# Moving gate blocks between the stages of a diffusion backbone block on one Trainium2 core

## Chip, core and metric

The kernel runs on one core of one Trainium2 chip. The metric is the device time of one execution in microseconds. The engines are TensorE (PE; its weight loads are shown as PEld), VectorE (DVE), ScalarE (ACT), GpSimd (POOL) and SyncE (SP), which here issues almost all DMAs. Each engine works through its own queue in order.

## What is computed

One layer of a hybrid block on 512 latent tokens and 256 context tokens of width 1024. The normed and modulated input `h` goes through one wide projection, whose columns feed three token mixers and the gates:

```python
proj = h @ w_in
p_qkv, p_z, p_ab, p_hy, p_lx, p_ly, p_gate = jnp.split(proj, offsets, axis=-1)
o_dn, ... = delta_net_branch(p_qkv, p_z, p_ab, ...)   # its output is multiplied by silu(p_z)
o_lru, ... = rglru_branch(p_lx, p_ly, ...)
o_hy = hyena_branch(p_hy, ...)
g_dn, g_hy, g_lru = jnp.split(jax.nn.sigmoid(p_gate), N_BRANCH, axis=-1)
merged = g_dn * (o_dn @ w_proj_dn) + g_hy * (o_hy @ w_proj_hy) + g_lru * (o_lru @ w_proj_lru)
```

After it come an output projection, a residual and a ConvFFN. The parts that matter here are `silu(p_z)` and the three sigmoid gates: 4 x 1024 output columns on the 512 latent tokens, in 32 blocks of 128 columns. They depend on `h` alone, so a block can stand anywhere between the norm and the place where its result is used.

## The kernel before

**Matrix products.** A float32 product is made from three products of a rounded high half and a low half (`mm3`, L173 to L175). A projection of one 128-column block (`load_w`, then `project`) loads 512 KB of weights on SP (L168), splits them into a high half (L155 on ACT or L157 on POOL) and a low half (L160, on DVE or POOL), and runs 8 x 3 matmuls of 128x512 for the latent tokens. Raw weights have three buffers, the high and low halves two each.

**Gate blocks.** `gate(z, m)` is one projection into a PSUM bank, one ACT operation from it (L574: Silu for z = 0, Sigmoid for z = 1, DeltaNet's gate; z = 2, Hyena's; z = 3, RG-LRU's), and one store of 256 KB to memory (L575). Later stages load the result. Of the 32 blocks, eight (z = 3) are in the RG-LRU loop. The 24 others are listed in `fill`: twelve stand beside the triangular solves, with the high half on ACT and the low half on POOL, and twelve in the scan, in halves of 12 matmuls.

**Stages around it.** After a prologue (to about 90 us) comes the RG-LRU loop over eight groups `g` of 128 channels (to about 345 us): `lru_in(g + 1)` (projection and convolution of the next group; its split writes the two halves of xs), `lru_gates(g)` (matmuls, eight sigmoids L518 and L519, four tanh L524 and L525), `gate(3, g)`, `lru_decay` (Exp L532 twice, L534 on DVE, L535 on POOL, L536 on ACT, L537 on DVE, square root L539 on ACT), `lru_scan` (L542, L544, L546, L547 on DVE), `lru_y` (L555 to L558), `lru_out` (L562 and L563 on POOL, then a split, L155 on ACT and L160 on DVE, 512 columns). Then come the merge, queries and keys. From about 530 us to 743 us two runs of triangular solves go on DVE, with a list of values and gate blocks (`work`) handed out beside them; `run` takes one item after every third step of the solve, and all that are left when the solve has ended. The second solve ends in matmuls of 32x32 (L853, L857). Then comes the DeltaNet scan of twelve steps (to about 950 us): four of context, eight of latent tokens. A step is L1005 (state times W and Q), L1015 (the triangular inverse), L1023 (the new state, taken up by DVE in L1028), L1035 (the output). A generator gives a half of a gate block at each of two places in a step: after L1015 and at the end. Beside it run the loads of w_mod (L1050), which DVE sums up (L1054); `mod_sum` turns these sums with a few small matmuls. Hyena, the projections and the FFN follow.

**Order.** A scheduler places the instructions of a stage on their engines by priority; in the prologue and on PE in the scan the order is that of the code. In the RG-LRU loop loads and splits of weights for later groups have a higher priority (`ahead`).

Of the kernel before, what the change touches and what calls it, by code (L numbers as in the profile page):

```python
# [17 lines left out]
P = 128  # L18
# [55 lines left out]
def tile_block(ctx: ExitStack, tc: tile.TileContext, I: dict, out: bass.AP, dbg=None, upto=99):  # L74
# [50 lines left out]
    act = nc.scalar.activation  # L125
# [51 lines left out]
    def project(w, outs):  # L177
        project_part(w, outs, 0, KD)
# [281 lines left out]
    mm, dn = Banks([0, 1, 2, 3]), Banks([4, 5, 6, 7])  # L460
# [67 lines left out]
    def lru_decay(gs, bufs):  # L528
        for g, (R, U, T4, T8) in zip(gs, bufs):
            for d in range(2):  # L530
                j = d * 8 + g
                act(R[:, d], R[:, d], AF.Exp, scale=nsp8[:, j:j + 1])  # L532
        for R, U, T4, T8 in bufs:
            stt(T4, R, 1.0, T4, op0=ALU.add, op1=ALU.mult)  # L534
            nc.gpsimd.tensor_scalar(R, T4, -1.0, 1.0, op0=ALU.mult, op1=ALU.add)  # L535
            act(T4, R, AF.Square)  # L536
            stt(T8, T4, 1.0, T8, op0=ALU.add, op1=ALU.mult)  # L537
        for R, U, T4, T8 in bufs:
            act(T8, T8, AF.Sqrt)  # L539
# [29 lines left out]
    def load_gate(z_, m, e_hi="pool", e_lo="dve"):  # L569
        return load_w(I["w_in"][GATES[z_][0] + m], e_hi=e_hi, e_lo=e_lo)  # L570
# [6 lines left out]
    def gate(z_, m, e_hi="pool", e_lo="dve"):  # L577
        w = load_gate(z_, m, e_hi, e_lo)
        pg = mm()
        project(w, [(pg, hh, hl)])  # L580
        gate_store(z_, m, pg)
# [16 lines left out]
    ksr, knr, kdr = ring(3, [143, 140]), ring(3, seq(146, 3, 2)), ring(3, seq(152, 3, 2))  # L598
    qsr, jkr = ring(2, seq(140, 2, 5)), ring(0.5, seq(158, 0.5, 4))
    atr = ring(1, [170, 171])  # L600
    NFILL = 12

    dcw = pv("dn_conv_w").rearrange("p (b j) -> p b j", j=4)
    kdd = dr.tile([2, TT, P, NH, P], F32, name="kdd")
# [25 lines left out]
    for g in range(8):  # L630
        ahead[0] = g > 0
        if 0 < g < 7:
            ins.append(lru_in(g + 1))
        bufs = lru_gates(g, *ins[g])
        gate(3, g)
        lru_decay([g], [bufs])
        lru_scan(*bufs)
        if g == 7:
            sqs.append(query(0))
        y, u = lru_y(g)  # L640
        lru_out(g, y, u, bufs[2])
        if g == 0:
            after(mark)
            if upto == 0:
                return
# [275 lines left out]
            if each and (not gens or n % EVERY == 0):  # L921
                each.pop(0)()

    fill = [(z_, m) for z_ in range(3) for m in range(8)]
    EVERY, NW1 = 3, 12
    vss = {}

# [5 lines left out]

    values = [lambda h=h: values_(h) for h in range(9)]
    ur = ring(2, [152, 154])
    gates = [lambda f=f: gate(*f, "act", "pool") for f in fill[:NFILL]]
    work = [w_ for p_ in zip(values, gates) for w_ in p_] + values[len(gates):] + gates[len(values):]
    run([solve_first(0), solve_first(1)], work[:NW1])
    run([solve_second()], work[NW1:])
# [12 lines left out]


    ur = ring(2, [186, 188])
    mm = Banks([0])
    o = at(60, [P, 4, NH, P])
    S = [at(84 + 4 * d, [P, NH, P]) for d in range(2)]
    war = ring(4, seq(92, 4, 4))
# [96 lines left out]

    def mod_sum(q):
        if q in (1, 2):
            mp = mm([P, 8])
            for b in range(8):
                mmul(mp[:, b:b + 1], acc[:, b * P:(b + 1) * P], ones[:, 0:1], start=True, stop=True)  # L1060
            vtt(mod34[:, q - 1], mp, pv("b_mod")[:, 16 + q * 8:24 + q * 8], op=ALU.add)
        else:
            row, brow = wr([1, D]), wr([1, D])
            load(brow, I["b_mod"][:, (2 + q) * D:(3 + q) * D])
            for b in range(2):
                mp = mm([1, 512])
                mmul(mp, ones[:, 0:1], acc[:, b * 512:(b + 1) * 512], start=True, stop=True)
                vtt(row[:, b * 512:(b + 1) * 512], mp, brow[:, b * 512:(b + 1) * 512], op=ALU.add)
            load(modr[0 if q == 0 else 1].unsqueeze(0), row)
# [9 lines left out]
    first_ins = len(bb.instructions)  # L1079
    halves = (None for z_, m in fill[NFILL:] for _ in gate_halves(z_, m))  # L1080
    ngap, FBM = 2 * (24 - NFILL), 1
    gap = 0
# [18 lines left out]
    mm, dn = Banks([0, 1, 2]), Banks([3, 4, 5, 6, 7])  # L1101
# [243 lines left out]
    mm = Banks([0, 1, 2, 3])  # L1345
# [263 lines left out]
```

## Time and profile before

| | us |
|---|---|
| median of 3 runs | 1673.54 (1671.61 to 1678.89) |
| profiled execution, its own time | 1676.85 |
| span of its trace | 1675.1 |
| PE busy | 1529.7 (91%) |
| DVE busy | 1195.7 (71%) |
| ACT busy | 615.7 (37%) |
| POOL busy | 589.3 (35%) |

The span is the time between the first and the last instruction of the trace. Busy shares are means over stages with different limits, so a stage is read by its own stretch of the trace: which engine is full there, and if none is, who waits for whom. In a row of a timeline the first number is the start in us, the second the duration; "x2" means that two operations were put together, and the bracket at the end gives the engine's idle time ahead of it and what ended it.

### The profile page before, as it was taken

Reading aid. Unit: us, or ns where it says so; the run is one execution under the profiler, and the core shown is the slowest. Engines: PE = TensorE matmul, PEld = TensorE weight load, DVE = VectorE, ACT = ScalarE, POOL = GpSimd, SP = SyncE. Lnnn points to the kernel's source line nnn. Section 1 sums busy time; section 2 is a strip of 40 time slices with the busy share of each in tenths; the row PEclk is TensorE's granted clock in tenths of the full one; section 3 lists DMA queues with packets and bytes.
Section 4 is the critical chain, followed back from the end, with each engine's and each line's share of the span. In section 5 each row is a group of like instructions: output and inputs, shape, how many; then the busy total and the mean of one; then the engine's idle time right before and its main releaser. Section 6 shows DMA issues by size and latency. Waiting matters only on the chain. (4 is left out here: it accounts for less than half of the span.)

```text
span 1675.1 us, 23659 instructions
## 1 busy us (share of the span) xinstructions
PE 1529.7 (91%) x9176; PEld 1258.0 (75%) x9176; DVE 1195.7 (71%) x1752; ACT 615.7 (37%) x1011; POOL 589.3 (35%) x401
## 2 busy tenths in 40 slices
PE   6899888889999899887999889999999999999998
PEld 2677777767887777775788678787888788888876
DVE  6877888756656997834666375777766899989873
ACT  4367787734553232320111330333222433333311
POOL 4653534325444360312434114222321233334441
PEclk9899999999999896878899999999999999999999
DMA  9432222335344332577888736322462223232331
GB/s 343 162 107 82 76 76 81 103 104 175 127 126 125 110 101 74 173 211 206 233 227 244 253 109 231 107 88 84 162 207 64 68 96 97 92 101 98 104 113 50
DMA packets 93056, 225.66 MB, mean 135 GB/s; under 512 B 9963, under 2 KB 30699, under 8 KB 92176
## 3 DMA queue, kind: packets, MB, share of 16 engines
q1 hardware_dynamic: 92112, 217.86, 41.6%
q0 software_dynamic: 832, 6.29, 0.9%
q8 instruction: 72, 1.18, 0.3%
q14 instruction: 40, 0.33, 0.1%
HBM read 190.45 MB, written 33.66 MB: 134 GB/s over the span
## 5 line engine op out<-in xcount | busy, mean ns | idle before, releaser
L173 PE MATMUL bank<-region,region 128*128 128x512 f32 (+1 forms) x2032 | 761.8, 376 | 28.9 <-DVE region L487 6.8
L175 PE MATMUL bank<-region,region 128*128 128x512 f32 (+1 forms) x2032 | 755.2, 373 | 25.1 <-DVE region L160 22.1
L174 PE MATMUL bank<-region,region 128*128 128x512 f32 (+1 forms) x2032 | 757.2, 373 | 4.2 <-DVE region L160 2.1
L173 PEld LDWEIGHTS bank<-region,region 128*128 128x128 f32 x2032 | 389.7, 192 | 106.8 <-ACT region L155 10.4
L175 PEld LDWEIGHTS bank<-region,region 128*128 128x128 f32 x2032 | 389.5, 192 | 98.6 <-DVE region L160 28.6
L174 PEld LDWEIGHTS bank<-region,region 128*128 128x128 f32 x2032 | 390.6, 192 | 69.0 <-DVE region L418 4.4
L160 DVE TENSOR_TENSOR region<-region,region 128x1024 fp32r<-128x1024 f32 (+2 forms) x241 | 268.7, 1128 | 174.1 <-ACT region L155 98.2
L155 ACT ACTIVATE region<-region 128x1024 fp32r<-128x1024 f32 (+2 forms) x209 | 178.4, 865 | 422.9 <-PE bank L174 132.8
L160 POOL TENSOR_TENSOR region<-region,region 128x1024 fp32r<-128x1024 f32 (+1 forms) x64 | 157.3, 2463 | 237.9 <-ACT region L155 200.4
L157 POOL TENSOR_SCALAR region<-region 128x1024 fp32r<-128x1024 f32 (+1 forms) x96 | 114.3, 1193 | 330.4 <-PE bank L174 147.7
L1423 DVE SCALAR_TENSOR_TENSOR region<-bank,pc,region 128x441 f32<-128x441 f32 (+2 forms) x352 | 224.8, 688 | 4.3 <-ACT region L1412 0.7
L485 DVE SCALAR_TENSOR_TENSOR region<-bank,pc,region 128x511 f32<-128x511 f32 (+1 forms) x56 | 34.1, 629 | 48.7 <-ACT region L482 45.8
L1054 DVE SCALAR_TENSOR_TENSOR region<-region,cc,region 128x1024 f32<-128x1024 f32 x28 | 41.7, 1488 | 33.9 <-DMA region<-in_w_mod_dram 33.4
L992 POOL TENSOR_TENSOR region<-region,region 128x512 f32<-128x512 f32 x32 | 49.1, 1564 | 39.5 <-DMA region<-rowd 36.8
L482 ACT ACTIVATE region<-bank,pc 128x512 f32<-128x512 f32 (+1 forms) x40 | 23.1, 597 | 98.6 <-PE bank L175 98.6
L1435 POOL TENSOR_TENSOR region<-region,region 128x512 f32<-128x512 f32 x22 | 34.3, 1561 | 66.3 <-DVE region L1423 52.3
L1028 DVE SCALAR_TENSOR_TENSOR region<-region,egl,bank 128x128 f32<-128x128 f32 x160 | 42.3, 339 | 21.3 <-PE bank L1023 21.3
L1005 PE MATMUL bank<-region,region 128*64 128x128 f32 x608 | 42.4, 306 | 9.2 <-DVE region L1028 9.2
L1005 PEld LDWEIGHTS bank<-region,region 128*64 128x64 f32 x608 | 39.8, 157 | 14.4 <-DVE region L1028 6.4
L1017 ACT ACTIVATE region<-bank 128x512 f32<-128x512 f32 x24 | 14.3, 598 | 89.9 <-PE bank L1015 89.9
L574 ACT ACTIVATE region<-bank 128x512 f32<-128x512 f32 x32 | 18.8, 588 | 70.6 <-PE bank L175 66.4
L1137 POOL TENSOR_TENSOR region<-region,region 128x512 f32<-128x512 f32 x8 | 12.2, 1523 | 85.6 <-DVE region L1121 85.6
(275 smaller groups left out, 1669.7 us busy)
## 6 DMA issues: line engine op xcount, KB each, us to landing
region<-in_w_in_dram SPq DMA_DIRECT2D x97, 512.0 KB, 3.9
region<-in_w_mod_dram SPq DMA_DIRECT2D x48, 512.0 KB, 6.2
region<-in_ffn_up_dram SPq DMA_DIRECT2D x44, 512.0 KB, 3.5
region<-in_w_proj_dram SPq DMA_DIRECT2D x24, 512.0 KB, 3.6
region<-in_ffn_down_dram SPq DMA_DIRECT2D x22, 512.0 KB, 3.5
gated<-region SPq DMA_DIRECT2D x32, 256.0 KB, 2.1
region<-gated SPq DMA_DIRECT2D x32, 256.0 KB, 4.0
kdd<-region SPq DMA_DIRECT2D x16, 384.0 KB, 2.8
```

The source lines that it names most:

```text
L155: act(hi, raw, AF.Copy)
L157: nc.gpsimd.tensor_scalar(hi, raw, 1.0, 0.0, op0=ALU.mult, op1=ALU.add)
L160: (vtt if e_lo == "dve" else gtt)(lo, raw, hi.bitcast(F32), op=ALU.subtract)
L173: mmul(ps, lh, rh, start=start, stop=False)
L174: mmul(ps, lh, rl, start=False, stop=False)
L175: mmul(ps, ll, rh, start=False, stop=stop)
L992: gtt(wq[d][:, hs], KQ[hf][:, :, chs[d] - 4], eg[:, hs].unsqueeze(2).to_broadcast([P, 4, 2, 64]), op=ALU.mult)
L1005: mmul(X[hf][rcs[d], h, :], wq[d][:, hf * 4 + h, kind], S[d][:, hf * 4 + h, :], start=(kind == 0 or h == 0), stop=(kind == 0))
L1028: stt(S[d][:, h], S[d][:, h], egl[:, d, c, i, h:h + 1], p3[hf][d][:, h % 4], op0=ALU.mult, op1=ALU.add)
L1054: stt(acc, w_, cc[:, k, 0:1], acc, op0=ALU.mult, op1=ALU.add)
L1423: stt(uv[:, ro, co], pv_[:, ri, ci], w[:, a * 3 + b:a * 3 + b + 1], uv[:, ro, co], op0=ALU.mult, op1=ALU.add)
L1435: gtt(uu[0], uu[0], uu[1], op=ALU.mult)
```

## The change

The list `fill` begins with z = 1 now. Its first eight blocks go into the RG-LRU loop, one in each iteration right behind `gate(3, g)`, with both halves of the weights split on POOL. The next ten (eight of z = 0, two of z = 2) stand beside the solves instead of twelve. Six are left for the scan instead of twelve; `ngap` follows from `NFILL`, so that a half comes only in every second place, the one at the end of a step. `mod_sum` writes to PSUM bank 1 instead of bank 0, which it shared with the gate halves.

```diff
-    NFILL = 12
+
+    NEARLY, NMERGE, NSOLVE = 8, 0, 10
+    NFILL = NEARLY + NMERGE + NSOLVE
+    fill = [(z_, m) for z_ in (1, 0, 2) for m in range(8)]
...
         gate(3, g)
+        if g < NEARLY:
+            gate(*fill[g], "pool", "pool")
         lru_decay([g], [bufs])
...
-    fill = [(z_, m) for z_ in range(3) for m in range(8)]
     EVERY, NW1 = 3, 12
...
-    gates = [lambda f=f: gate(*f, "act", "pool") for f in fill[:NFILL]]
+    gates = [lambda f=f: gate(*f, "act", "pool") for f in fill[NFILL - NSOLVE:NFILL]]
...
-    mm = Banks([0])
+    mm, mm1 = Banks([0]), Banks([1])
...
-            mp = mm([P, 8])
+            mp = mm1([P, 8])
...
-                mp = mm([1, 512])
+                mp = mm1([1, 512])
```

Lines behind the first of these places have a number some 3 to 5 higher in the changed kernel (L853 is L858 there, L1017 is L1021).

On ACT in the RG-LRU loop, before: the end of one group's tanh (L524, L525), with the copy of xs (L155, 128x768) and the out-copy (L155, 128x512) among them, the gate's sigmoid (L574), and the decay.

```order
L155 ACTIVATE region_800<-region_83 128x768
L525 ACTIVATE region_1068<-region_1065,sp_744 128x768
L524 ACTIVATE region_1067<-region_1065,sp_745 128x768
L155 ACTIVATE region_106<-region_1353 128x512
L525 ACTIVATE region_1068<-region_1065,sp_744 128x768
L574 ACTIVATE region_1491<-bank_63 128x512
L532 ACT_TABLE_LOAD
L532 ACTIVATE region_1065<-region_1065,nsp_746 128x768 x2
L555 ACTIVATE region_992<-bank_64 128x512
L557 ACT_TABLE_LOAD
L557 ACTIVATE region_992<-region_992 128x512
L536 ACTIVATE region_1067<-region_1065 128x1536
```

The same place in the changed kernel, from the first sigmoids (L518, L519) of the group to its first tanh:

```order
L518 ACTIVATE region_1095<-bank_69,pc 128x256
L518 ACTIVATE region_1096<-bank_69,pc 128x256
L519 ACTIVATE region_1095<-bank_70,pc 128x512
L155 ACTIVATE region_106<-region_1441 128x512
L519 ACTIVATE region_1096<-bank_67,pc 128x512
L518 ACTIVATE region_1095<-bank_68,pc 128x256
L519 ACTIVATE region_1095<-bank_69,pc 128x512
L518 ACTIVATE region_1096<-bank_68,pc 128x256
L519 ACTIVATE region_1096<-bank_70,pc 128x512
L524 ACTIVATE region_1097<-region_1095,sp_745 128x768
```

The out-copy has moved from a place behind all sigmoids and three of the tanh to one behind three sigmoids. And on ACT from the last tanh of that group on, in the changed kernel:

```order
L525 ACTIVATE region_1098<-region_1095,sp_744 128x768
L532 ACT_TABLE_LOAD
L532 ACTIVATE region_1095<-region_1095,nsp_746 128x768
L574 ACT_TABLE_LOAD
L574 ACTIVATE region_1163<-bank_66 128x512
L532 ACT_TABLE_LOAD
L532 ACTIVATE region_1095<-region_1095,nsp_746 128x768
L574 ACT_TABLE_LOAD
L574 ACTIVATE region_1193<-bank_63 128x512
L536 ACTIVATE region_1097<-region_1095 128x1536
L555 ACTIVATE region_1022<-bank_64 128x512
L539 ACT_TABLE_LOAD
```

The two gates' operations (L574) now stand between and behind the two Exps, each with a table load of its own, and the square root's table load comes right behind L555.

On ACT at the end of the solves, before: the last gate blocks (L155 splits their weights, L574 is their Silu or Sigmoid) ahead of the first copies L854 of the second solve's matmuls.

```order
L155 ACTIVATE region_697<-region_436 128x1024
L574 ACT_TABLE_LOAD
L574 ACTIVATE region_3961<-bank_63 128x512
L155 ACTIVATE region_437<-region_696 128x1024
L574 ACTIVATE region_4084<-bank_64 128x512
L574 ACTIVATE region_3961<-bank_65 128x512
L574 ACTIVATE region_4084<-bank_66 128x512
L854 ACTIVATE region_4852<-bank_67 32x512
```

The same place in the changed kernel (L897 copies a value, L859 is L854 before):

```order
L155 ACTIVATE region_437<-region_696 128x1024
L574 ACTIVATE region_4316<-bank_66 128x512
L897 ACTIVATE region_3393<-bank_69 128x256
L897 ACTIVATE region_3393<-bank_70 128x512
L574 ACT_TABLE_LOAD
L574 ACTIVATE region_4193<-bank_63 128x512
L574 ACTIVATE region_4316<-bank_64 128x512
L859 ACTIVATE region_5084<-bank_67 32x512
```

Of the four blocks behind the last value, two are left.

On PE in a latent step of the scan, before, from L1015 over the half block (12 matmuls, of which the last five stand here) to L1023:

```order
L1015 MATMUL bank_65<-region_1354,region_5718 64x128 x8
L1015 MATMUL bank_66<-region_2456,region_5718 64x128 x8
...
L174 MATMUL bank_63<-region_81,region_437 128x512
L175 MATMUL bank_63<-region_80,region_438 128x512
L173 MATMUL bank_63<-region_80,region_437 128x512
L174 MATMUL bank_63<-region_81,region_437 128x512
L175 MATMUL bank_63<-region_80,region_438 128x512
L1023 MATMUL bank_69<-region_1175,region_5480 128x128
L1023 MATMUL bank_70<-region_1175,region_5480 128x128
```

The same place in the changed kernel (L1019 is L1015 before, L1027 is L1023):

```order
L1019 MATMUL bank_65<-region_1442,region_5753 64x128 x8
L1019 MATMUL bank_66<-region_2688,region_5753 64x128 x8
L1027 MATMUL bank_69<-region_1235,region_5571 128x128
L1027 MATMUL bank_70<-region_1235,region_5571 128x128
L1027 MATMUL bank_69<-region_1235,region_5571 128x128
L1027 MATMUL bank_70<-region_1235,region_5571 128x128
```

The half is gone from between them; the one at the end of a step stays.

## Rows read from the trace of the kernel before

**Rows 1.** The page: its head, and what the DMAs moved in 40 slices.

```profile
span 1675.1 us, 23659 instructions
GB/s 343 162 107 82 76 76 81 103 104 175 127 126 125 110 101 74 173 211 206 233 227 244 253 109 231 107 88 84 162 207 64 68 96 97 92 101 98 104 113 50
```

**Rows 2.** Stretches: us, busy time of PE, PEld, DVE, ACT, POOL, PEclk, DMA share, GB/s.

```profile
145.00:290.00 145.00, 128.28 (x629) 104.23 (x627) 121.57 (x110) 109.46 (x139) 62.78 (x38) 1.00 0.25 80
199.50:226.80 27.30, 24.31 (x121) 19.83 (x121) 23.30 (x22) 21.16 (x28) 11.73 (x7) 1.00 0.23 77
700.00:743.00 43.00, 35.41 (x358) 30.56 (x358) 20.54 (x16) 13.46 (x20) 9.28 (x5) 0.78 0.69 199
743.00:811.00 68.00, 52.76 (x452) 41.68 (x452) 36.80 (x70) 9.23 (x16) 15.84 (x14) 0.87 0.76 212
811.00:950.00 139.00, 132.47 (x1474) 112.35 (x1475) 80.07 (x167) 18.93 (x33) 50.93 (x36) 0.95 0.84 231
1450.00:1500.00 50.00, 50.00 (x222) 41.40 (x221) 44.09 (x66) 18.78 (x25) 18.88 (x9) 1.00 0.31 104
```

**Rows 3.** Timeline of ACT in the RG-LRU loop, 199 to 236 us.

```profile
207.21 0.63 ACT L155 ACTIVATE region<-region 128x512 fp32r<-128x512 f32 x1 [4.19 <-POOL region L563]
...
209.18 1.28 ACT L532 ACT_TABLE_LOAD   x1
210.47 1.77 ACT L532 ACTIVATE region<-region,nsp 128x768 f32<-128x768 f32 x2
...
223.07 1.26 ACT L519 ACTIVATE region<-bank,pc 128x512 f32<-128x512 f32 x2
...
226.08 0.97 ACT L524 ACTIVATE region<-region,sp 128x768 f32<-128x768 f32 x1
...
234.61 0.63 ACT L155 ACTIVATE region<-region 128x512 fp32r<-128x512 f32 x1 [4.20 <-POOL region L563]
```

**Rows 4.** Timeline of DVE in the same stretch.

```profile
212.27 1.76 DVE L534 SCALAR_TENSOR_TENSOR region<-region,region 128x1536 f32<-128x1536 f32 x1 [1.66 <-ACT region L532]
...
222.05 1.74 DVE L542 TENSOR_TENSOR region<-region,region 128x1536 f32<-128x1536 f32 x1
...
230.27 3.16 DVE L160 TENSOR_TENSOR region<-region,region 128x1024 fp32r<-128x1024 f32 x2
```

**Rows 5.** Timeline of POOL in the same stretch.

```profile
230.50 2.12 POOL L562 TENSOR_TENSOR region<-region 128x512 f32<-128x512 f32 x1 [2.42 <-ACT region L524]
232.69 1.89 POOL L563 TENSOR_TENSOR region<-region,region 128x512 f32<-128x512 f32 x1
```

**Rows 6.** Timeline of POOL beside the solves, 580 to 620 us.

```profile
582.95 13.91 POOL L160 TENSOR_TENSOR region<-region,region 128x1024 fp32r<-128x1024 f32 x2 [8.29 <-ACT region L155]
...
616.44 2.40 POOL L160 TENSOR_TENSOR region<-region,region 128x1024 fp32r<-128x1024 f32 x1 [3.97 <-ACT region L155]
```

**Rows 7.** Timeline of PE behind the RG-LRU loop, 336 to 344 us.

```profile
342.70 0.39 PE L667 MATMUL bank<-ident,region 32*128 32x32 f32 x2 [5.94 <-ACT region L662]
```

**Rows 8.** Timelines of DVE, PE and ACT at the end of the second solve.

```profile
711.24 2.07 DVE L839 STREAM_TRANSPOSE region<-region 32x1024 f32<-32x1024 f32 x1
...
725.93 1.26 PE L853 MATMUL bank<-region,region 32*32 32x32 f32 x34
...
726.09 0.60 ACT L574 ACTIVATE region<-bank 128x512 f32<-128x512 f32 x1 [4.84 <-PE bank L175]
```

**Rows 9.** Timeline of the scan's context steps, 786 to 797 us, all engines.

```profile
792.17 1.04 POOL L157 TENSOR_SCALAR region<-region 128x1024 fp32r<-128x1024 f32 x1 [5.17 <-DMA region<-in_w_in_dram]
793.25 1.23 DVE L160 TENSOR_TENSOR region<-region,region 128x1024 fp32r<-128x1024 f32 x1 [2.60 <-POOL region L157]
...
795.05 2.19 PE L1005 MATMUL bank<-region,region 128*64 128x128 f32 x18 [6.01 <-DVE region L1028]
```

**Rows 10.** Timeline of a latent step of the scan, 848 to 860 us, PE.

```profile
851.71 1.96 PE L1015 MATMUL bank<-region,region 64*64 64x128 f32 x32
...
856.55 2.06 PE L1023 MATMUL bank<-region,region 64*128 64x128 f32 x32
```

## Prediction

> **What bounds the kernel now.** Read the page first. The span is 1675.1 us and the profiled execution took 1676.85 us; the 1.75 us between them lie outside the program and stay. The sum is made against that execution; the median of the three runs shown, 1673.54 us, is 3.3 us lower, and the sum is carried over to it unchanged.
>
> Next, the table of stretches [rows 2]: in the tail of the program (1450 to 1500) TensorE (PE) is busy for all of 50.00 us, so whatever the stages before give or lose passes through to the end. Three of them hold gate blocks that the change moves. In the RG-LRU loop, 27.3 us for one of the eight channel groups hold PE 24.31, DVE 23.30, ACT 21.16: no engine is full. From 700 to 743 PE is busy 35.41 of 43 us; in the scan 52.76 of 68 us (context steps) and 132.47 of 139 (latent steps).
>
> Then the ACT queue of the loop [rows 3]. The copy that makes the high half of the branch's output (L155, 512 columns; the out-copy from here on) starts at 207.21 and at 234.61, 27.40 us apart, and both times ACT has waited 4.2 us for POOL's L563. So the loop is set by a chain through all engines: out-copy, sigmoid of the gate and Exp on ACT (210.47), L534 on DVE (212.27), L535 to L542 (222.05) [rows 4], the scans, POOL's L562 and L563 (230.50, 232.69) [rows 5], out-copy. It reaches the end: at 342.70 PE has stood 5.94 us for an ACT copy, L662, that is queued behind the last out-copy [rows 7].
>
> **Price of a gate block.** 222 matmuls of 512 columns took 50.00 us [rows 2], 0.225 us each; a block has 24 of them, 5.4 us of PE. On ACT it adds a sigmoid of 0.6 us [rows 8], on SP two issues (a load of 512 KB, a store of 256 KB), and two splitting operations that now go to POOL: 1.04 us for the high half [rows 9], 2.40 for the low half where DVE leaves POOL alone, and 13.91 for two, 7 each, beside the solves [rows 6].
>
> **Part 1, eight blocks into the loop.** If PE were the limit, eight blocks would cost at most 43 us, and a period could not fall below 24.31 + 5.4 = 29.7 us. But the chain is what counts, and the ACT order changes on it at two places. First, the out-copy of the group before is now queued after three of the eight sigmoids of the next group, where it came after all of them and most of the tanh. So ACT's work that today fills the time before the copy has to wait behind it. Second, the new gate's sigmoid parts the two Exps, so that three table loads stand ahead of the second Exp instead of one.
>
> I count from the end of the out-copy to L534. Before: 234.61 less 27.40 is 207.21, plus 0.63 is 207.84; L534 starts at 212.27: 4.4 us. After: five sigmoids, which with one more take 226.08 - 223.07 = 3.0 us before [rows 3], so 2.4; four tanh and the copy of xs, some 0.85 each by L524's 0.97 less its overlap with the next, 4.2; three table loads at 1.28, 3.85; a sigmoid 0.6; two Exps 1.77 [rows 3]. That is 12.9 us, **8.5 more**. From L534 to L542 it is now 9.8 us [rows 4]; afterwards the table load of the square root stands before the wait, with no convolution work between, and it lies under DVE's L537: 8.4 is my estimate, 1.4 less. From L542 to the end of the out-copy it is now 13.2 us; afterwards DVE does its third scan before the rest of the convolution and the split: 11.5, 1.7 less. The period becomes 27.4 + 8.5 - 1.4 - 1.7 = 32.8 us, 5.4 more, over the 29.7 that PE needs. Six periods of that are 32 us, and the last, which has no convolution to wait for, I put at 3: **+35 us**, and PE passes it on at L662. The bounds are 7 x (29.7 - 27.3) = +17, if ACT's waits close up until PE is the limit, and +57 (the third rival). I take the chain, since its rows are the ones that PE waits for. POOL's new work (3.4 us a block, 8 at the worst price) lies between L563 and L535, some 15 us; SP's sixteen issues lie in a stretch with a DMA share of 0.25 [rows 2]; but the two stores of a period now wait on SP for the second gate sigmoid, 13 us after the out-copy, and the next loads stand behind them. Three raw weight buffers are filled ahead, 16 us of PE, so I cost that at nothing; without that cover a load comes late in each period, which the upper bound takes in.
>
> Table loads are where the Trainium skill speaks against the change. At 209.18 the load takes 1.28 us, and the Exp starts at 210.47, right behind it [rows 3]. The Trainium skill, "ScalarE: Activation LUTs", section "What ACT_TABLE_LOAD costs", adds a drain of about 1.38 us to every switch; the two more loads on the chain would then cost 2.8 us a period more, some 19 us in all. The trace shows no such gap, and I leave it out.
>
> **Part 2, ten blocks beside the solves instead of twelve.** The order moves nothing until the end, where four blocks run in a row, and after the change two. DVE finishes its part of the second solve at 711.24 + 2.07 = 713.3; PE comes to L853, which needs it, at 725.93, right behind the last block, whose sigmoid is at 726.09 [rows 8]. Two blocks less are 2 x 5.4 = **-11 us**, to 715.1, still 1.8 us behind DVE, so nothing else becomes late by the rows. The bounds are -5, if the loads or POOL's splits hold up the earlier blocks, and -12.6, DVE's finish. The loads of w_mod that were fetched there, at 199 GB/s [rows 2], start as much earlier.
>
> **Part 3, six blocks in the scan instead of twelve.** Every step had a half block between L1015 and L1023 and another after L1035; the first goes. L1015 ends at 851.71 + 1.96 = 853.7 and L1023 starts at 856.55 [rows 10]; between them PE did the half, 2.9 us. L1023 needs ACT's copies of L1015's two results (L1017), and the first of them can be made while the second result is still computed, so hardly anything on PE's own path fills that gap again: twelve halves are 35 us, the best case. Against it stand the loads. The scan moves 212 and 231 GB/s at shares of 0.76 and 0.84 [rows 2], 46.5 MB. Six blocks take 4.7 MB from that: 1.6 MB at 212 GB/s and 3.1 MB at 231 are **21 us**, if the scan goes with its bytes. DVE shows how loads reach PE: a half's raw weights came late (POOL waited 5.17 us, 792.17), the split followed on DVE (793.25), and L1028 behind it in the same queue held PE for 6.01 us (795.05) [rows 9]. Such waits belong to the load order, and fewer blocks don't remove all of them. I take **-25**, nearer to the bytes than to PE. The worst case counts the blocks as cheap bytes, at the highest rate of the page, 343 GB/s [rows 1]: -14. mod_sum's new bank frees it from the gate's bank at four places; it waits instead for L1028 to have read bank 1, for which L1005 right behind it waits anyway: I cost that at nothing.
>
> **Sum.** +35 - 11 - 25 = -1: 1675.9 in terms of the profiled execution, **1672.5 us** in terms of the median.
>
> **The rivals.** *The loop is held by PE after all.* Then ACT's out-copy doesn't wait, since the chain has room, and part 1 costs 17: 1654.5. For it: PE is the busiest engine there, at 24.31. Against it: the 4.2 us that ACT waits each time. 12%.
>
> *The scan goes down to PE's floor*, -35: 1662.5. For it: latent steps leave PE idle for 6.5 of 139 us only. Against it: a DMA share of 0.84. 15%.
>
> *POOL's splits hold up DVE.* In the loop two DVE splits beside POOL's L562 took 3.16 us (230.27) [rows 4], 1.58 each against 1.23 [rows 9], and L562 itself 2.12; beside the solves a split of POOL takes 7 us instead of 2.4 [rows 6]. After the change POOL starts the new block's splits right behind L563, while DVE does the out-split, the rest of the convolution and, behind them, what ACT's xs copy waits for; that copy has hardly 0.3 us to spare in the count above. If DVE stands for all of POOL's 1.04 + 2.40 us, 3.1 come through in each of seven periods, +22: 1694.5, slower. It decides from about 1 us a period. Against it: DVE's operations grew by 0.35 us, not by POOL's whole time. 10%. The Trainium skill, "SBUF — State Buffer" section "SBUF: two separate sides",, calls the port that both use an exclusive lock for a whole instruction, where DVE reads two operands from SBUF; the 7 us agree with that for POOL.
>
> *The scan stays with its loads*, -14: 1683.5, slower. For it: DVE and POOL wait for loads there (5.17 us at 792.17), and PE without a half to do waits in its place. 17%.
>
> That the blocks don't move is excluded by the order. **Chances and range.** My forecast has 46%. 0.5% (8.4 us) is about what a measurement of this kernel can tell from no change: the edges are 1665.2 and 1681.9. Faster: 12 + 10 of the 15 + 7 of my own = 29%. Slower: 10 + 12 of the 17 + 4 = 26%. The rest, 45%, is within. The range holds the forecast, the scan's two cases and the edge of the first rival: 1654 to 1692.
>
> **What would show it.** In the loop the out-copies should stand 32 to 33 us apart, with five sigmoids behind each and no wait of ACT for PE; 29 to 30 apart with PE full is the first rival, 35 or more with longer DVE splits the third. PE's wait for the last out-copy, which ends at 342.70 now, should end near 378. L858 (L853 before) should start within 2 us of DVE's last transpose. The scan, from there to the end of its last state update, should be 25 us shorter; PE's time between L1019 and L1027 should be near zero. I am wrong if ACT finds room for the sigmoids before the out-copy, or if clock or loads in the scan take back the halves.

## The result, and the profile after

The changed kernel took 1701.1 us (median of 4 runs, 1698.07 to 1707.22) against 1674.68 us before (4 runs, 1671.61 to 1678.89): a ratio of **1.0138**, 95% interval 1.011 to 1.0167. By the ratio it is slower by some 23 us (the two medians are 26 apart), where 1672.5 was forecast and 1692 was the upper end. The profiled execution has a span of 1701.0 us, 25.9 more than before [rows 1]. The sums below are made between the two profiled executions.

The stretches of the changed kernel that answer to [rows 2], in the same columns: one whole stretch of the RG-LRU loop, one period of it, the end of the solves, context and latent steps of the scan, and 50 us of the tail.

```profile
145.00:290.00 145.00, 133.35 (x634) 110.53 (x633) 98.38 (x92) 110.50 (x137) 68.56 (x41) 0.98 0.28 91
199.50:232.50 33.00, 30.46 (x144) 25.35 (x144) 22.31 (x22) 24.38 (x31) 15.25 (x9) 0.95 0.26 88
742.00:776.00 34.00, 23.93 (x310) 21.12 (x310) 21.76 (x20) 10.25 (x16) 3.44 (x2) 0.75 0.59 171
776.00:842.00 66.00, 50.99 (x528) 42.23 (x530) 36.33 (x74) 9.23 (x16) 13.55 (x13) 0.82 0.79 224
842.00:979.00 137.00, 104.38 (x1248) 90.03 (x1244) 68.57 (x157) 15.99 (x26) 38.27 (x31) 0.86 0.78 206
1475.00:1525.00 50.00, 50.00 (x222) 41.38 (x221) 44.07 (x66) 18.06 (x24) 18.91 (x9) 1.00 0.32 101
```

The tail is as full as before. The scan is the surprise: its latent steps take 137 us where they took 139, with 28 us less of PE's busy time in them, and TensorE's granted clock fell from 0.95 to 0.86.

To see where time goes, I compare the start of the same instruction in both traces: the first transpose behind the loop (L667, now L672), the first of the keys' squares (L760, L765), DVE's last transpose of the solves (L839, L844), the last 32x32 product (L853, L858), and the first transpose of Hyena (L1141, L1145).

| place | before | after | shift | of that in the part |
|---|---|---|---|---|
| first transpose behind the RG-LRU loop | 342.7 | 380.1 | +37.4 | +37.4 loop |
| first of the keys | 449.4 | 491.6 | +42.2 | +4.8 merge and queries |
| DVE's last transpose of the solves | 711.2 | 756.3 | +45.1 | +2.9 keys and solves |
| last 32x32 product | 735.0 | 768.5 | +33.5 | -11.6 end of the solves |
| first transpose of Hyena | 976.6 | 1001.3 | +24.7 | -8.8 scan |
| span | 1675.1 | 1701.0 | +25.9 | +1.2 the rest |

**The loop.** ACT, DVE and POOL in one period of the changed kernel (the places of [rows 3 to 5]):

```profile
211.18 0.63 ACT L155 ACTIVATE region<-region 128x512 fp32r<-128x512 f32 x1 [6.02 <-POOL region L563]
...
218.32 1.28 ACT L532 ACT_TABLE_LOAD   x1
...
220.57 1.28 ACT L574 ACT_TABLE_LOAD   x1
...
222.48 1.28 ACT L532 ACT_TABLE_LOAD   x1
223.78 0.94 ACT L532 ACTIVATE region<-region,nsp 128x768 f32<-128x768 f32 x1
...
244.23 0.63 ACT L155 ACTIVATE region<-region 128x512 fp32r<-128x512 f32 x1 [5.94 <-POOL region L563]
```

```profile
211.84 0.86 DVE L160 TENSOR_TENSOR region<-region,region 128x512 fp32r<-128x512 f32 x1 [1.43 <-ACT region L155]
...
224.75 1.76 DVE L534 SCALAR_TENSOR_TENSOR region<-region,region 128x1536 f32<-128x1536 f32 x1 [5.11 <-ACT region L532]
226.43 1.22 DVE L160 TENSOR_TENSOR region<-region,region 128x1024 fp32r<-128x1024 f32 x1
...
233.85 1.76 DVE L542 TENSOR_TENSOR region<-region,region 128x1536 f32<-128x1536 f32 x1 [0.95 <-ACT region L539]
```

```profile
212.24 2.73 POOL L160 TENSOR_TENSOR region<-region,region 128x1024 fp32r<-128x1024 f32 x1
...
226.59 2.39 POOL L535 TENSOR_SCALAR region<-region 128x1536 f32<-128x1536 f32 x1 [3.38 <-DVE region L534]
```

The out-copies are 33.05 us apart (32.8 in the prediction) and ACT waits 6 us for each of them. From the out-copy's end at 211.81 to L534 it is 12.9 us, as summed; from there to L542 9.1 (8.4 summed); from there to the next out-copy's end at 244.86 11.0 (11.5 summed).

**The scan.** The largest waits of PE and of POOL, each first before (743 to 977 us), then after (776 to 1002 us). The columns: who waited and for whom, us in total, times, the longest.

```profile
PE bank L1005 <- DVE region L1028: 9.2, 3, 6.0
PE bank L1015 <- DVE region L1009: 6.6, 3, 4.5
...
POOL region L992 <- DMA region<-rowd: 36.8, 7, 11.5
```

```profile
PE bank L1009 <- POOL region L996: 37.0, 12, 7.3
PE bank L1071 <- DVE region L1072: 5.9, 2, 5.1
...
POOL region L996 <- DMA region<-rowd: 82.9, 8, 27.2
```

L996 (L992 before) is POOL's product that makes W and Q for a step from the rows `rowd`; L1009 (L1005) is the step's first product on PE. Before, PE seldom waited for that product, since it still had half blocks to do when the rows came. With the half between L1019 and L1027 gone, PE comes to the next step's first product earlier, and there it waits for POOL, 37 us in all, and POOL for the rows.

### The profile page after: what moved, and what is told of

It reads as the page before. It is cut to its first block, busy times and chain, and to the rows that moved or that the text cites. A ratio compares the mean times of both kernels' runs of the same rounds, so it can differ in the third digit from the quotient of the medians.

```text
span 1701.0 us, 23683 instructions
## 1 busy us (share of the span) xinstructions
PE 1541.7 (91%) x9176; PEld 1274.6 (75%) x9176; DVE 1183.8 (70%) x1746; ACT 632.9 (37%) x1024; POOL 597.8 (35%) x409
## 5 line engine op out<-in xcount | busy, mean ns | idle before, releaser
L160 DVE TENSOR_TENSOR region<-region,region 128x512 fp32r<-128x512 f32 (+1 forms) x235 | 264.7, 1137 | 166.8 <-ACT region L155 100.1
L155 ACT ACTIVATE region<-region 128x1024 fp32r<-128x1024 f32 (+2 forms) x207 | 176.5, 864 | 426.2 <-PE bank L174 129.8
L160 POOL TENSOR_TENSOR region<-region,region 128x1024 fp32r<-128x1024 f32 (+1 forms) x70 | 174.2, 2494 | 231.2 <-ACT region L155 195.6
L1009 PE MATMUL bank<-region,region 128*64 128x128 f32 x608 | 51.5, 334 | 37.4 <-POOL region L996 37.0
L1009 PEld LDWEIGHTS bank<-region,region 128*64 128x64 f32 x608 | 46.5, 174 | 45.7 <-POOL region L996 42.4
L996 POOL TENSOR_TENSOR region<-region,region 128x512 f32<-128x512 f32 x32 | 41.5, 1327 | 82.9 <-DMA region<-rowd 82.9
L1021 ACT ACTIVATE region<-bank 128x512 f32<-128x512 f32 x24 | 14.3, 597 | 140.6 <-PE bank L1019 136.5
L1439 POOL TENSOR_TENSOR region<-region,region 128x512 f32<-128x512 f32 x22 | 34.4, 1562 | 66.4 <-DVE region L1427 59.6
L1013 DVE TENSOR_TENSOR region<-region,bank 128x512 f32<-128x512 f32 x22 | 14.8, 685 | 39.0 <-PE bank L1009 34.3
L534 DVE SCALAR_TENSOR_TENSOR region<-region,region 128x1536 f32<-128x1536 f32 x8 | 14.8, 1854 | 37.9 <-ACT region L532 37.9
```

The lines of the kernel that those rows point to most:

```text
L155: act(hi, raw, AF.Copy)
L160: (vtt if e_lo == "dve" else gtt)(lo, raw, hi.bitcast(F32), op=ALU.subtract)
L996: gtt(wq[d][:, hs], KQ[hf][:, :, chs[d] - 4], eg[:, hs].unsqueeze(2).to_broadcast([P, 4, 2, 64]), op=ALU.mult)
L1009: mmul(X[hf][rcs[d], h, :], wq[d][:, hf * 4 + h, kind], S[d][:, hf * 4 + h, :], start=(kind == 0 or h == 0), stop=(kind == 0))
L1439: gtt(uu[0], uu[0], uu[1], op=ALU.mult)
```

## Experiments

Runs of one group share the runs of the kernel before. "Behind the loop" is the start of the first transpose behind the RG-LRU loop, "scan" the time from the scan's first product (L1015 in the kernel before) to Hyena's first transpose, both in us from one trace of each kernel. The scan varies by itself: with the scan of the kernel before it was 233.2 and 228.4 us (before, dup_lru), with that of the changed kernel 224.6, 219.3 and 232.2 (after, d_first, p_first). So a difference under some 13 us between the scans of two single traces is no finding; the ratios rest on several runs each.

| kernel | ratio to before | 95% interval | behind the loop | scan |
|---|---|---|---|---|
| after | 1.0138 | 1.011 to 1.0167 | 380.1 | 224.6 |
| dup_lru | 1.0238 | 1.0196 to 1.0279 | 379.9 | 228.4 |
| scan6 | 0.9942 | 0.9914 to 0.9969 | 343.4 | 221.5 |
| d_first | 1.0071 | 1.005 to 1.0092 | 364.2 | 219.3 |
| p_first | 1.0213 | 1.0181 to 1.0246 | 386.6 | 232.2 |
| r_high | 1.021 | 1.0168 to 1.0252 | 379.4 | 230.6 |
| r_four_high | 1.023 | 1.0198 to 1.0262 | 380.7 | 234.4 |
| nomod | 0.9903 | 0.9872 to 0.9934 | 379.1 | 178.9 |
| mod_small | 0.9942 | 0.9917 to 0.9967 | 380.4 | 187.7 |
| mod_short | 1.0114 | 1.007 to 1.0158 | 379.8 | 217.5 |
| mod_late | 1.0093 | 1.0061 to 1.0126 | 364.3 | 160.1 |
| mod_hy | 0.9916 | 0.9883 to 0.9948 | 367.4 | 159.9 |
| mod_split | 0.9869 | 0.9843 to 0.9896 | 367.5 | 178.1 |

### The loop's part alone: dup_lru

```diff
         gate(3, g)
+        gate(1, g, "pool", "pool")
         lru_decay([g], [bufs])
```

> The kernel before, with eight gate blocks computed once more in the RG-LRU loop, where the change puts them (they are computed again in their old places, so everything behind the loop is as before). It shows what the loop's part costs alone. Theory 1 (a chain over all engines, ACT's queue in it): out-copies 33 us apart, +37 us at the last out-copy, +40 to +43 us in all, since PE loses behind the loop the wait that it had there: 1715 to 1718. Rival (PE holds the loop): out-copies under 30.5 us apart, +17 to +22: 1692 to 1697. The sum of the prediction had +35: 1709.

1717.29 us against 1678.92: +38, and by the ratio +40 (33 to 47). The out-copies were 33.05 us apart, and the first transpose behind the loop came at 379.9. So the loop's part costs what theory 1 says, some 5 more than the prediction's +35; the rival's 17 to 22 is out.

### The scan's part alone: scan6

```diff
-    halves = (None for z_, m in fill[NFILL:] for _ in gate_halves(z_, m))
-    ngap, FBM = 2 * (24 - NFILL), 1
+    halves = (None for z_, m in fill[NFILL:18] for _ in gate_halves(z_, m))
+    ngap, FBM = 12, 1
...
-        load(th, gated[2, m])
+        load(th, gated[2, m % 2])
```

> The kernel before with six gate blocks in the scan instead of twelve, in every second place, and the sums of w_mod in bank 1; six of Hyena's gate blocks are left out and others are read in their place. It shows what the scan's part gives alone. Theory 2 (a step waits for its own row loads, which SP issues late, so that PE idles where the halves stood): the scan's own length within 6 us of before, in all -2 to -10. Rival bytes: -21. Rival PE's floor: -35. The prediction had -25.

1669.6 us: a ratio of 0.9942, -10 us (-5 to -14). Six blocks with 32 us of PE's work went out of the kernel altogether, and it lost 10. Bytes at the scan's mean rate (-21) and PE's floor (-35) are out; the fourth rival's -14 is at the edge. The scan of its trace is 11.7 us shorter than before, where theory 2 had 6 at most. PE's new wait is here too, with nothing changed ahead of the scan:

```profile
PE bank L1005 <- POOL region L992: 27.9, 10, 6.5
```

That the time fits theory 2 doesn't yet show that the late issue of the rows is the cause.

### The order on ACT: d_first and p_first

d_first puts the early gate ahead of lru_gates in the code and makes a group's output behind lru_gates of the next; p_first does the first alone.

```diff
+    held = []
     for g in range(8):
...
+        if g < NEARLY:
+            gate(*fill[g], "pool", "pool")
         bufs = lru_gates(g, *ins[g])
+        if held:
+            lru_out(*held.pop())
         gate(3, g)
-        if g < NEARLY:
-            gate(*fill[g], "pool", "pool")
...
-        lru_out(g, y, u, bufs[2])
+        held.append((g, y, u, bufs[2]))
```

> The changed kernel, where in the loop the early gate block stands ahead of lru_gates and the output of a group is made after lru_gates of the next group in the code. This puts the order on ACT back: the out-copy behind the tanh, both Exps together, four table loads in a group instead of six; PE, POOL and DVE do the same work as in the changed kernel. Theory 1 (the ACT order lengthens the chain): out-copies 29.5 to 31 us apart instead of 33, in all -14 to -24 against the changed kernel, 1677 to 1687. Rival (POOL's splits hold DVE up, or PE's work counts in full wherever it stands): 33 us apart as in the changed kernel, 1698 to 1703.

> The changed kernel with the early gate block ahead of lru_gates in the code, and the output of a group left where it was. On ACT both Exps stand together again and a group has four table loads, but the out-copy stands ahead of all eight sigmoids of the next group. It parts the two causes in the ACT order. Theory 1 by the terms of the sum: from the out-copy's end to L534 11.7 us instead of 12.9, a period of 31 to 32.5 us, in all -4 to -14 against the changed kernel. If the table loads were the whole cause, the period would be 29.7 to 30.5, as in d_first; if the out-copy's place were, 33 as in the changed kernel.

d_first has 1.0071 against the 1.0138 of the changed kernel, 11 us of it regained (the forecast had 14 to 24). ACT and then PE's stretches (columns of [rows 2]) in its loop:

```profile
218.00 0.61 ACT L155 ACTIVATE region<-region 128x512 fp32r<-128x512 f32 x1
...
219.12 1.28 ACT L532 ACT_TABLE_LOAD   x1
220.41 1.77 ACT L532 ACTIVATE region<-region,nsp 128x768 f32<-128x768 f32 x2
...
249.05 0.62 ACT L155 ACTIVATE region<-region 128x512 fp32r<-128x512 f32 x1
```

```profile
199.50:232.50 33.00, 32.81 (x164) 27.55 (x163) 23.49 (x22) 23.16 (x29) 12.93 (x9) 1.00 0.34 111
232.50:265.50 33.00, 31.16 (x147) 25.88 (x147) 23.81 (x22) 23.60 (x32) 13.38 (x9) 0.95 0.28 92
```

The out-copies are 31.05 us apart, ACT no longer waits for POOL at them, and PE is close to full: a loop near the first rival's (29 to 30 us) appears. The first transpose behind the loop comes 15.9 us earlier than in the changed kernel, so the order of the code is worth that much of the 37; the other 21.5 remain with the same blocks in the better order. The edit gives PE, DVE and POOL another order too, so that the whole of the 15.9 comes from ACT is argued from the rows and not shown by itself.

p_first should have kept a part of the gain, by the count; it was slower than the changed kernel, with out-copies 34.2 to 34.5 us apart in the middle of the loop. DVE in it:

```profile
231.20 1.76 DVE L534 SCALAR_TENSOR_TENSOR region<-region,region 128x1536 f32<-128x1536 f32 x1 [1.57 <-ACT region L532]
...
238.32 0.69 DVE L160 TENSOR_TENSOR region<-region,region 128x512 fp32r<-128x512 f32 x1 [2.12 <-POOL region L157]
238.93 1.75 DVE L537 SCALAR_TENSOR_TENSOR region<-region,region 128x1536 f32<-128x1536 f32 x1
...
242.24 1.76 DVE L542 TENSOR_TENSOR region<-region,region 128x1536 f32<-128x1536 f32 x1 [1.56 <-ACT region L539]
```

The out-copy ended at 218.78, so L534 came 12.4 us later: two table loads less on the way saved half a microsecond, since all eight sigmoids stand there now. And from L534 to L542 it is 11.0 us, not 8.4, because a weight split of POOL and then one of DVE stand ahead of L537. So taking away two table loads doesn't shorten the period as long as the out-copy stands ahead of the sigmoids. How much the out-copy's place and the parted Exps are worth alone isn't shown: p_first made the first worse while it mended the second, and d_first mends both.

### Earlier rows: r_high and r_four_high

```diff
+        egs = [None] * 2
+        for d in range(2) if s else ():
+            egs[d] = egr([P, NH, 64])
+            with tc.high_priority():
+                load(egs[d], rowd[1, d, chs[d]].partition_broadcast(P))
         v, kd, wa = chunk_loads(s, lat)
         wq = [None] * 2
         for d in range(2) if s else ():
-            eg = egr([P, NH, 64])
-            load(eg, rowd[1, d, chs[d]].partition_broadcast(P))
+            eg = egs[d]
```

> The changed kernel with the row loads of a scan step issued ahead of its other loads and at a higher priority; bytes, blocks and buffers are the same. Theory 2 (late issue of the row loads on SP): POOL's L996 waits for rowd for less than half of 83 us, PE's L1009 for POOL less than half of 37 us, and the scan is 12 to 22 us shorter: 1679 to 1689. Rival (the DMAs are full, whatever the order): the waits move to other loads and the time stays, 1697 to 1703.

r_four_high takes four buffers instead of `egr`'s two in the latent steps.

> The changed kernel with the row loads of a scan step ahead and at a higher priority, as in r_high, and four buffers for them instead of two in the latent steps, so that SP does not stand behind POOL's use of the old rows. If SP's head-of-line wait for the two buffers (60 us in r_high) is what took r_high's gain away: the wait under 20 us and the scan 10 to 20 us shorter than in the changed kernel, 1681 to 1691. If the loads as a whole hold the scan (theory 3: what SP can issue and the DMAs can land of one step's 2 MB, w_mod's 512 KB blocks among them): PE's wait moves on to the sums of w_mod or to vd and wad, and the time is 1698 to 1713.

Neither is faster than the changed kernel; by the ratios, 1.021 and 1.023, both are slower. In both PE's wait for POOL is gone from the list, and new ones stand there; the largest of PE and of SP in r_high's scan, and that of SP in r_four_high's (L1013 is L1005 before, L1068 the small products of w_mod's sums, L1062 DVE's additions, L991 the issue of the rows, L1000 POOL's product from them):

```profile
PE bank L1068 <- DVE region L1062: 19.6, 2, 11.3
PE bank L1023 <- DVE region L1017: 9.0, 5, 3.7
```

```profile
SPq L991 <- POOL region L1000: 60.5, 12, 15.7
```

```profile
SPq L991 <- POOL region L1000: 65.8, 12, 15.1
```

Theory 2's remedy falls: with the rows ahead, SP stands for POOL, which still reads the old rows, w_mod comes later, and PE waits for its sums. r_four_high was to take that wait of SP away (under 20 us) and didn't: it is 65.8 us with four buffers. So it doesn't tell what room for more rows would give, and an order with the rows early and SP free was not tried. In both orders that were tried, another load is late: that is what theory 3 says.

### What the loads wait for: nomod, mod_small, mod_short

nomod leaves out most of the loads and additions of w_mod; mod_small makes the loads small; mod_short makes the additions short. mod_late, below, moves them all. The edits of nomod, mod_small and mod_short, in that order:

```diff
-        for k in range(4) if s_ % 3 < 2 else ():
+        for k in range(1) if s_ % 3 == 0 else ():
```

```diff
-        load(w_, I["w_mod"][k * P:(k + 1) * P, (2 + q) * D:(3 + q) * D])
+        load(w_[:, 0:128], I["w_mod"][k * P:(k + 1) * P, (2 + q) * D:(2 + q) * D + 128])
```

```diff
-            stt(acc, w_, cc[:, k, 0:1], acc, op0=ALU.mult, op1=ALU.add)
+            stt(acc[:, 0:64], w_[:, 0:64], cc[:, k, 0:1], acc[:, 0:64], op0=ALU.mult, op1=ALU.add)
```

> The changed kernel with 28 of the 32 loads of w_mod in the scan left out, and the additions that use them; blocks, step loads and their order otherwise stay. Theory 3 (the step's loads queue behind w_mod's on SP and in the DMAs): POOL's L996 waits little for rowd, PE's L1009 waits under 10 us for POOL, a latent step takes 11 to 13 us, and the scan is 35 to 55 us shorter than the changed kernel's, 1645 to 1666. Rival (each step's own chain of rows, POOL, PE and DVE sets 16 us): scan shorter by less than 15, 1686 to 1701.

> The changed kernel, where each of the 32 loads of w_mod in the scan brings 64 KB instead of 512 KB; the count of loads, their places on SP, the buffers that they wait for and DVE's 32 full additions stay (the sums are then not w_mod's). It parts w_mod's bytes from its places in the queues. If the bytes hold the scan (the step's own loads wait behind them in the DMAs): nearly the gain of nomod (28 loads and additions left out), the scan 30 to 46 us shorter than in the changed kernel, 1655 to 1671. If the places on SP or DVE's additions hold it: under 12 us shorter, 1689 to 1701.

> The changed kernel with all 32 loads of w_mod whole, but 28 of DVE's additions over 64 columns instead of 1024 (0.2 instead of 1.3 us each; the sums are then not w_mod's). It takes 30 us of work from DVE in the scan and leaves the bytes. If the bytes hold the scan: under 8 us shorter than the changed kernel, 1693 to 1703. If DVE's queue holds it: 15 to 30 us shorter, 1671 to 1686.

nomod's scan is 46 us shorter than the changed kernel's, mod_small's 37, mod_short's 7, which is within the spread. All three lengths and times came out as theory 3, or the bytes, had them; only POOL's own wait for the rows in nomod, 34.2 us, is not as little as was expected. The whole scan as one stretch (columns of [rows 2]) of the kernel before, the changed one, mod_small and mod_short, one fence each:

```profile
743.40:976.60 233.20, 205.31 (x2006) 169.84 (x2006) 130.25 (x250) 46.29 (x122) 70.00 (x51) 0.93 0.78 223
```

```profile
776.70:1001.30 224.60, 175.43 (x1858) 147.97 (x1858) 117.14 (x244) 42.78 (x116) 54.48 (x46) 0.86 0.77 217
```

```profile
778.80:966.50 187.70, 163.25 (x1857) 139.32 (x1857) 123.99 (x242) 42.62 (x116) 61.45 (x46) 0.93 0.72 189
```

```profile
774.90:992.40 217.50, 174.07 (x1858) 147.94 (x1858) 93.17 (x244) 42.77 (x116) 52.28 (x46) 0.87 0.79 224
```

mod_short took 24 us of DVE's work out of the scan (117.14 to 93.17) and PE still waits 37.5 us for POOL there. mod_small left every load and addition in its place, and with 1/8 of w_mod's bytes POOL's wait for the rows fell from 82.9 to 35.4 us:

```profile
POOL region L996 <- DMA region<-rowd: 35.4, 8, 8.6
```

So it is the size of w_mod's loads, not their count nor DVE's additions, that makes the step's loads late. Where they are late is read from more rows: from issue to landing, the row loads (L991) of the changed kernel, of mod_small and of nomod took

```profile
DMA to landing us min/median/max: 3.5/5.4/7.8
```

```profile
DMA to landing us min/median/max: 3.6/4.0/4.4
```

```profile
DMA to landing us min/median/max: 3.4/5.5/8.8
```

With nearly all of w_mod gone (nomod) they land no faster than with all of it, yet PE's wait for POOL's rows is gone there. So most of the delay comes before the issue, on SP. SP between two pairs of row loads of the changed kernel, and its wait with a w_mod load until an earlier one has landed, in the changed kernel and then in mod_small:

```profile
870.34 1.00 SPq L991 DMA_DIRECT2D region<-rowd  x2
871.45 11.91 SPq L1054 DMA_DIRECT2D region<-in_w_mod_dram  x4
...
897.52 0.87 SPq L991 DMA_DIRECT2D region<-rowd  x2
```

```profile
SPq L1054 <- DMA region<-in_w_mod_dram: 25.8, 6, 6.8
```

```profile
SPq L1054 <- DMA region<-in_w_mod_dram: 7.8, 3, 3.7
```

An issue of such a load alone takes some 0.4 us; four of them hold SP for 11.91, and the loads of the next step stand behind them. In the rest of these 27 us SP stands for a weight buffer and for a gate block's store. This part is read from the rows; no run parts the standing of SP from the bytes that cause it.

The price: 26 of the 32 loads are issued in the scan's stretch, 448 KB less each, 11.9 MB; with all 32 it is 14.7 MB. 37 us for them are 2.5 to 3.1 us per MB.

The four rows also show the clock. mod_small and the changed kernel do the same products in the scan (1857 and 1858 records), but PE is busy for 163.25 us in the one, at a granted clock of 0.93, and for 175.43 in the other, at 0.86, where it also stands idle for 49 us instead of 24. The changed kernel's scan against the one before is 29.9 us less of busy time and 21.3 more of idle time.

### A version that is faster than both: mod_late, mod_hy, mod_split

All three are d_first with w_mod moved. mod_late puts four loads and additions behind each merge of DeltaNet's output; mod_hy one or two there and one behind each projection of Hyena's second to fourth quarter; mod_split leaves half in the scan and spreads the other half. mod_late also gives Hyena fewer scratch buffers. The edit of mod_hy against d_first, with parts left out:

```diff
-        if s_ % 3 == 2:
-            mod_sum(s_ // 3)
...
-        for k in range(4) if s_ % 3 < 2 else ():
-            mod_part(s_ // 3, s_ % 3 * 4 + k)
...
+    def mod_next(n=1):
+        for q, k in parts[:n]:
+            mod_part(q, k)
+            if k == 7:
+                mod_sum(q)
+        del parts[:n]
...
                 conv3(dst, ps, off + g)
+                if qr:
+                    mod_next()
...
+        mod_next(1 + (m > 1))
```

> d_first, with all loads and sums of w_mod moved from the scan to the eight merges of DeltaNet's output behind it, where the DMAs have a share of about 0.3; Hyena has three scratch buffers instead of five. Theory 3: the scan is 35 to 55 us shorter than in d_first, and of that the merges give back DVE's 42 us of sums only in part: 1645 to 1680. Rival (the sums and loads only change place): 1685 to 1700.

> d_first with the loads and sums of w_mod taken out of the scan and spread over the stages behind it, one or two to each merge of DeltaNet's output and one to each projection of Hyena's second to fourth quarter, with all scratch buffers in place. In mod_late the scan took 160 us where d_first took 219, but 65 us came back in the crowded merges. If thin spreading hides them (PE is busy for 95% there and the DMA share is 0.3 to 0.6): 1635 to 1655, faster than both kernels. If each still costs its slot of the raw weight buffers and its 1.3 us on DVE: 1675 to 1695.

> mod_hy with half of w_mod's loads and sums back in the scan, two at the end of eight of its steps, and the other 16 spread over the merges and Hyena's projections. In mod_hy the scan lost 59 us against d_first and the stages behind it got 35 longer (244.5 instead of 209 us from the first to the last of Hyena's transposes). If the cost of w_mod in the scan rises steeply only once the loads pass what PE's time covers, half of it there costs less than half of 59, and half of 35 is saved behind: 1650 to 1663, faster than mod_hy. If both costs go with the bytes: 1665 to 1672.

mod_late lost 59 us of scan and gave 65 back behind it (274.2 us from the first to the last of Hyena's transposes, 209.2 in d_first): 1.0093, and the rival's time. Spread thinly (mod_hy) it was 244.5 us behind, and the kernel is faster than both, 0.9916, though the forecast of 1655 at most fell. mod_split is the best by its median, 1657.6 us, as forecast, and by its ratio, **0.9869** (0.9843 to 0.9896), though the interval overlaps mod_hy's. Its scan and what is behind it:

```profile
767.40:945.50 178.10, 159.43 (x1837) 135.63 (x1837) 98.33 (x225) 42.64 (x116) 53.39 (x45) 0.96 0.85 224
945.50:1168.10 222.60, 207.99 (x1019) 173.97 (x1020) 159.88 (x190) 54.98 (x78) 55.55 (x40) 0.95 0.46 152
```

Together 400.7 us, against 404.4 in mod_hy and 428.5 in d_first. The first 16 loads taken out of the scan gave 41 us of the 59, the next 16 only 18, by one trace of each. PE's wait for POOL's rows, 36.6 us in d_first's scan, is 8.7 in mod_split's and not in mod_hy's list.

## Why the prediction was wrong

- **The loop: the mechanism was right, the sum a little short.** The chain held it, ACT's queue lengthened it, and the two places were the ones named: 33.05 us against 32.8, 37.4 at the wait behind the loop against 35. The way from the out-copy to L534 came out term by term (12.9); the two parts behind it missed by +0.7 and -0.5, and that they nearly cancel is luck. d_first shows that the order is worth 15.9 of the 37.4: the same blocks in the better order still cost 21.5 there, where PE is close to full. The +0.7 between L534 and L542 has its row: POOL's L535 took 2.39 us beside DVE's L160 that had begun 0.16 us before it. The Trainium skill, "SBUF — State Buffer", section "SBUF: two separate sides", says that the loser of the shared port waits for the other's whole instruction; 1.06 us of waiting and the 1.5 us that L535 takes in p_first are about the 2.39, so this row agrees. The third rival as it was put didn't come: DVE's out-split beside POOL's new splits took 0.86 us where it took 0.69 in p_first, not 3 us more, and the xs copy was not late.
- **What the sum left out behind the loop: +7.7.** I carried the +35 on as it was. By the keys it was 42.2, at the solves' end 45.1. From the first transpose to the keys PE was busy 106.34 of 111.5 us at a granted clock of 0.95, before 102.48 of 106.7 at 0.98; about 1 us of it are eight small products that stood ahead of that transpose before. It repeats: dup_lru has 111.4 us between the two places. What lowered the clock there wasn't tried, and the 2.9 between the keys and DVE's last transpose stay open.
- **The end of the solves: right.** -11.6 against -11. PE's L858 starts at 759.19, within 1 us of DVE's last transpose.
- **The scan: the step that failed.** The prediction took -25, between the bytes at the scan's mean rate (21) and PE's floor (35), and called 14 the worst case. The traces give -8.8, and scan6 alone -10 (-5 to -14), the firmer of the two. Two things were mis-sized. The mean rate was the wrong price of a large load: if the blocks' bytes cost what w_mod's do (2.5 to 3.1 us per MB in mod_small), their 4.7 MB are worth 12 to 15, an estimate near the fourth rival's price at 343 GB/s. And the halves were read as work in the way of PE, where they stood over a wait: PE's wait for POOL's rows isn't among its larger ones before, when PE had 2.9 us more of gate to do in each step. With the halves gone it is 37 us; other waits shrank, so PE's idle time in the scan grew by 21.3. The clock took its part as well: the products that are left take 12 us more of PE than in mod_small. How much of those 12 us the scan's length feels isn't shown. The prediction had named both ("if clock or loads in the scan take back the halves") and gave the clock no term. The new bank of mod_sum, put at nothing, cost PE little: its waits at L1071 (L1067) are 8.2 us instead of 4.0. The fourth rival had the mechanism of the wait ("PE without a half to do waits in its place"), with 17%.
- **The sum of it:** +37.4 + 7.7 - 11.6 - 8.8 + 1.2 = 25.9. With the scan at -25 it would have been 10, still over the forecast by the 7.7 and the loop's 2.4.
- Table loads: behind each load the next operation starts at once, as at 223.78, and the count with 1.28 us for a load met the way to L534. The second price, that of the Trainium skill ("ScalarE: Activation LUTs", "What ACT_TABLE_LOAD costs"), which adds a drain to every switch, isn't seen in these rows either.

What stays open: how the 16 us between the changed order and d_first divide between the out-copy's place and the parted Exps, how much of the scan's loss is the clock's, and whether an order of SP's queue exists that keeps both the rows and w_mod in time.

## What to carry to other kernels

Work that fills an engine between two products may stand over a wait that no list of waits shows; before it is taken away, look for what arrives during it, and count that as the next thing to be late. In this scan, with a DMA share near 0.8, removing matmuls gave back no more than their bytes, and moving loads that have time (w_mod) out of it gave more than the two other orders of loads that were tried. Look also at what the issuing engine stands for: a load that is late may have been issued late. In a loop that is bound by a chain, read the instruction order of every engine on the chain: a block of 5.4 us of PE cost 5.6 us a period in the changed order, and 3.6 in d_first's.

## What the runs showed of the hardware that was not expected

- Putting a step's two row loads (256 KB each) ahead of its others in SP's queue made the kernel no faster, and by the ratios some 0.7% slower (r_high 1.021 against 1.0138): SP then stood 60.5 us for the buffer's reader.
- The row loads took a median of 5.4 us from issue to landing beside 512 KB loads of w_mod, and 5.5 with nearly all of these left out (nomod); what differed was when SP issued them.
- The same scan code took 224.6, 219.3 and 232.2 us in three kernels whose earlier stages differed, while the loop's period was 33.03 to 33.06 us in each turn of the changed kernel and of dup_lru: the stage that waits for loads repeats badly.
